# Residual of the down pass in five parts, recurrence rows loaded during attention, gate transposes in the other bank ring

## The chip, the cores and the metric

The kernel runs on one core of a Trainium2 chip. The core has five engines with an instruction stream each: TensorE (PE, matrix products), VectorE (DVE), ScalarE (ACT), GpSimd (POOL) and SyncE (SP), which here issues the DMA transfers. The metric is the device time of one execution in microseconds, the median over several runs.

## The reference

Two layers of a flow-matching backbone over 1024 latent tokens and a prefix of 256 context tokens, each of width 1024. In each layer half of the heads are a bidirectional matrix-memory recurrence (mLSTM) with its own gates, and half are a two-dimensional neighbourhood attention; both read one combined input projection and share one output projection. A squared-ReLU MLP with 4096 hidden features follows. Cut to what matters:

```python
for l in range(DEPTH):                                   # 2 layers
    need_ctx = l < DEPTH - 1                             # the context is not needed after layer 0
    h  = rmsnorm(x, norm1_g[l]) * (1.0 + sc1) + sh1      # scales and shifts from c (or c_ctx)
    hc = rmsnorm(xc, norm1_g[l]) * (1.0 + sc1c) + sh1c
    y, yc = token_mixers(h @ w_in[l], hc @ w_in[l], ...) # y: recurrence rows, then attention rows
    x = x + g1 * (y @ w_out[l])
    h = rmsnorm(x, norm2_g[l]) * (1.0 + sc2) + sh2
    x = x + g2 * (square(relu(h @ w_mlp1[l])) @ w_mlp2[l])
    # the same for xc with yc, if need_ctx
return rmsnorm(x, final_g)
```

In the recurrence, the gates of all tokens (four per head: input and forget, forwards and backwards) are accumulated along the tokens before anything can be weighted by them.

## The kernel before, in words

All products are made in three parts: each fp32 operand is split into a rounded part (`hi`, an ACT cast) and the rest (`lo`, a subtraction on DVE or POOL), and `mm3` (L94 to L96) adds hi x hi, hi x lo and lo x hi. Features lie on the 128 partitions, tokens along the free axis. The 1280 tokens are three groups: group 0 is the context (256 tokens), groups 1 and 2 are 512 latent tokens each. A product over the 1024 features takes eight k-tiles.

PSUM banks come from two rings: `mm` with 2 banks and `q` with 6, taken by `bank(tag)`. Whoever takes the next bank of a ring waits until its last reader is done. SBUF tiles come from pools in the same way: `wraw` (2 buffers) takes weights and rows as they land, `yraw` (2 buffers) takes rows during attention, and `raw` (6 buffers) takes the operands of the down pass. Within each engine, instructions run in a fixed order that a scheduler derives from the order in which the code is written; only the opening is ordered by hand.

A layer goes through these stages:

- **Keys, values and gates.** `mlstm_kv` projects tile by tile; ACT copies the values out of the bank (`va`, L497), DVE rotates the keys (L450 to L454), PE transposes them (L507). `gates` transposes the gate rows (L318) in three groups of 4, 4 and 2 tiles, and DVE adds the biases (L319, L320). From there a chain on DVE and ACT leads through the scans to `wc` (L364) and `st` (L374), which PE reads in L384 and L394. Value products of the attention heads stand between L318 and L384 on PE and cover the chain.
- **Recurrence, then attention.** The recurrence's output rows are stored to memory (`yscr`), k-tiles 0 to 3; attention's rows are k-tiles 4 to 7. Attention runs over pairs of heads and query tiles: scores (L986, L996), a fused maximum on DVE (L991, L997), the exponential on ACT (L1001), scaling on DVE (L1003), transposes on PE (L1014, L1025, L1038), copies by ACT and DVE, and the products with the values (L1048). Between these pieces the generator `ahead` already makes half of the output projection of the first group: it loads the group's rows with `load_y` (a DMA, an ACT cast at L1057, a subtraction at L1058) and runs four output tiles with a `residual` each (L1062). The first group is group 0 in layer 0, group 1 in layer 1.
- **Output projection.** `outproj` loads the eight k-tiles of each remaining group by `load_y` through `wraw`, then the weights of the output projection through the same two buffers.
- **Up and down.** The MLP uses products of sums of operands (seven instead of eight, named "1" to "7"). The down pass `run` goes through 56 steps in layer 0 (seven products of eight steps); each step is 24 matmuls of 512 columns, and operands are prepared four steps ahead (`AHEAD = 4`): DMA into `raw`, cast (L1098) and subtraction (L1099). At step 2 the function `load` brings in the whole residual `x` from memory (`xmid`), in pieces of 0.5 MB (context) and 1 MB (latent). The last step of each product adds banks to the residual (`take`): the first product needs the first half of group 1's features at step 7, the second needs the second half of group 2's at step 15, the third needs group 2's first half and group 1's second at step 23, and the context needs its own at the end.

The lines quoted are numbered as in the profile.

Of the kernel before, what the change touches and what calls it, by code (L numbers as in the profile page):

```python
# [26 lines left out]
KT = D // 128  # L27
# [10 lines left out]
def fview(a):  # L38
    return a.bitcast(F32)
# [8 lines left out]
class Kern:  # L48
# [81 lines left out]
    def load(self, pool, name, shape, src=None):  # L130
        t = pool.tile(shape, F32, name=name)
        self.nc.sync.dma_start(t[:], self.d[name] if src is None else src)
        return t
# [171 lines left out]
    def gates(self, l, tp_):  # L305
        nc, d = self.nc, self.d
# [6 lines left out]
        yield  # L313
        for c0 in range(0, NT, 4):
            nch = min(4, NT - c0)
            acc, ts = self.bank("mm"), slice(c0 * 128, (c0 + nch) * 128)
            for c in range(nch):
                nc.tensor.transpose(acc[:, c * 128:(c + 1) * 128], self.gr[:, c0 + c, :, :].rearrange("p q h -> p (q h)"), self.ident)  # L318
            nc.vector.tensor_scalar(ig[:, ts], acc[0:64, :nch * 128], self.bgate[l][:, 0:1], None, ALU.add)  # L319
            nc.vector.tensor_scalar(fg[:, ts], acc[64:128, :nch * 128], self.bgate[l][:, 1:2], None, ALU.add)  # L320
            yield
# [67 lines left out]
        for si, st in ((1, st2), (0, st1)):  # L389
            for c0 in range(0, NT, 4):  # L390
                nch = min(4, NT - c0)
# [499 lines left out]
    def ahead(self, l, gi, xsrc, yh, yl, W, xt):  # L891

        g0, n = GROUPS[gi]
        raw = []

        def fetch():
            raw.append(self.wp.tile([128, 1024], F32, name="wraw", bufs=WRAW))
            self.nc.sync.dma_start(raw[-1][:], self.d["w_out"][l, len(raw) - 1])

        for _ in range(WRAW):  # L900
            fetch()
        yield
        for i in range(WB):
            W.append(self.split_raw(raw[i], 1024))
            if len(raw) < WB:
                fetch()
            self.load_y(l, gi, yh, yl, range(2 * i, min(2 * i + 2, KT - 1)), self.np_)
            yield
        for f in range(WB):
            t = self.ap.tile([128, 512], F32R, name="ah2", bufs=KT)  # L910
            xt.append(fview(t[:, :n]))
            self.nc.sync.dma_start(xt[f], xsrc[f * 128:(f + 1) * 128, g0:g0 + n])
        self.load_y(l, gi, yh, yl, range(KT - 1, KT), self.np_)
        yield
        for f in range(WB):
            self.residual(gi, f, self.out_tile(f, gi, yh, yl, W[f]), 16, self.mod, xt[f])
            yield

    def out_tile(self, f, gi, hi, lo, w):
# [131 lines left out]
    def load_y(self, l, gi, hi, lo, ks=range(KT), pool=None):  # L1051
        nc = self.nc
        g0, n = GROUPS[gi]
        for k in ks:
            y = pool.tile([128, 512], F32, name="yraw", bufs=2) if pool else self.wp.tile([128, 1024], F32, name="wraw", bufs=WRAW)
            nc.sync.dma_start(y[:, :n], self.yscr[l][k * 128:(k + 1) * 128, g0:g0 + n])
            nc.scalar.copy(hi[k][gi][:], y[:, :n])  # L1057
            (nc.vector if gi == 2 or k == KT - 1 else nc.gpsimd).tensor_sub(lo[k][gi][:], y[:, :n], fview(hi[k][gi][:]))  # L1058

    def residual(self, gi, f, acc, row, mod, xs):  # L1060
        v = 1 if gi == 0 else 0
# [7 lines left out]
    def outproj(self, l, x, xsrc, groups, hi, lo, W=(), xt=()):  # L1069

        done = groups[0] if xt else -1
        for f0 in range(0, KT, WB):
            W = list(W) if f0 == 0 else []
            for gi in groups:
                if f0 == 0:
                    if gi == done:
                        self.load_x(x, xsrc, (gi,), (1,))
                        for f, t in enumerate(xt):
                            self.nc.scalar.copy(xf(x, gi, f), t)
                        continue  # L1080
                    self.load_y(l, gi, hi, lo)
                    self.load_x(x, xsrc, (gi,))
                if not W:
                    run_all(self.w_out(l, f0, W))
                for f in range(f0, f0 + WB):
                    self.residual(gi, f, self.out_tile(f, gi, hi, lo, W[f - f0]), 16, self.mod, xf(x, gi, f))
                    yield
# [255 lines left out]
    def down(self, l, hid, we, alloc):  # L1343

        nc, d = self.nc, self.d
# [111 lines left out]
        def run(x, mod, load, after, filler):  # L1457
            todo = iter(())
            for n in range(4, AHEAD):
                prepare(n)  # L1460
            for n, (p, b, s) in enumerate(whole):
                if n == 2:
                    load()
                if s == 0:
                    banks[p] = banks[ONTO[p]] if p in ONTO else [self.bank("mm") for _ in range(4)]
                w, h = ready.pop(n)
                for z in range(2):
                    for f in range(4):
                        multiply(banks[p][f][:], f, w[z], h[z], 512, p not in ONTO and s == z == 0, s == NS - 1 and z == 1)
                prepare(n + AHEAD)  # L1470
                next(todo, None)
                if n > 2 and n % 2:
                    next(filler, None)
                if s == NS - 1:
                    for f in range(4):
                        take(p, x, mod, f)
                    if p in "72":
                        run_all(todo)
                        alloc(2 if p == "7" else 1)
                        todo = after(2 if p == "7" else 1, 0, 512)  # L1480
            if not final:
                context(x, mod, todo, filler)
                alloc(0)
                run_all(after(0, 0, GROUPS[0][1]))
                return

            p, b = SEQUENCE[-1]
            banks[p], W, H = [self.bank("mm") for _ in range(4)], {}, {}

            def halves(o, k0):  # L1490
                r = raw()
                nc.sync.dma_start(r[:].rearrange("p (j t) -> p j t", j=4), hid["b"][HID.index(b), k0:k0 + 4, :, o:o + 256].rearrange("j p t -> p j t"))
                for z in range(4):
                    k = k0 + z
                    H[o, k] = (act("ah0", 256), act("al0", 256)) if o and k < KT else (act("ah1"), act("al1"))
                    self.parts(r[:, z * 256:z * 256 + 256], H[o, k][0][:, :256], H[o, k][1][:, :256])

            def chunk(i):
                halves(0, 4 * i)
                for s in (2 * i, 2 * i + 1):  # L1500
                    W[2 * s], W[2 * s + 1] = weights(p, s, s < 4)

            chunk(0)
            for i in range(4):
                if i < 3:
                    chunk(i + 1)
                for k in range(4 * i, 4 * i + 4):
                    for f in range(4):
                        multiply(banks[p][f][:, 0:256], f, W[k], H[0, k], 256, k == 0, k == 15)
                    next(todo, None)  # L1510
            run_all(todo)
            for i in range(4):
                halves(256, 4 * i)
            for f in range(4):
                take(p, x, mod, f, 0, 256)
            todo = after(1, 0, 256)
            q = self.bank("mm")

            def square(f, first=False, stop=False):
                sq = self.sp.tile([128, 512], F32, name="tmp", bufs=self.ntmp)  # L1520
                nc.scalar.activation(sq[:, :256], xf(x, 1, f, 256, 256), AF.Square)
                nc.tensor.matmul(q[:, :256], self.ones[:], sq[:, :256], start=first, stop=stop)

            for f in range(4):
                for k in range(16):
                    multiply(banks[p][f][:, 256:], f, W[k], H[256, k], 256, k == 0, k == 15)
                    if k % 4 == 3:
                        next(todo, None)
                square(f + 4, f == 0)
                if f:  # L1530
                    square(f - 1)
                take(p, x, mod, f, 256, 256)
            square(3, stop=True)
            run_all(todo)
            run_all(after(1, 256, 256, (q, 256)))
# [176 lines left out]
    def run(self):  # L1712
        nc, d = self.nc, self.d
        PS = bass.MemoryType.PSUM
        with self.open(name="pad", side="right") as pad, self.open(name="const") as self.cp, self.open(name="w") as self.wp, \
# [13 lines left out]
            hi, lo = self.alloc_act()  # L1729
# [3 lines left out]
            for l in range(DEPTH):  # L1733
                need_ctx = l < DEPTH - 1
                groups = (0, 1, 2) if need_ctx else (1, 2)
                yh, yl, W, xt = self.mixers(l, xsrc, hi, lo, need_ctx, W, accs, Wv if l == 0 else [])
# [82 lines left out]
                with self.open(name=f"xd{l}") as xp, self.open(name=f"sd{l}") as self.sp, self.open(name=f"we{l}") as wx:  # L1819
# [1 line left out]
                    self.wide, self.ntmp = 1, 3  # L1821
                    x = self.alloc_x(xp, groups)

                    def load():
                        self.load_x(x, xmid, groups)

                    if l == DEPTH - 1:
                        finish(x, mod, load, lambda *a: self.final(x, *a), ada)
# [66 lines left out]

RAWS = 6
AHEAD = 4
HID = ("11", "21", "22", "T1", "T2", "T3", "T4")


# [109 lines left out]
```

## Time and profile before

| | |
|---|---|
| median of 3 runs | 2866.62 us (2863.16 to 2868.66) |
| the profiled execution's own time | 2864.0 us |
| its span | 2862.2 us |
| mean granted clock of PE | 0.996 |
| PE busy | 2812.3 us (98%) |
| DVE, ACT, POOL busy | 2206.3 us (77%), 1267.9 us (44%), 105.4 us (4%) |
| DMA | 497.40 MB, mean 174 GB/s |

Every time stamp is counted in microseconds from the start of the span. A row of the timeline gives start, duration, engine, line, operation, what it writes and reads, and in brackets the idle time of the engine before it with what ended it. Gaps of PE are where time can be won or lost; the other engines count only where PE waits for them. The table's GB/s is a mean: in some stages the transfers stand at several times zero or near their highest rate, so a stage has to be looked at by itself.

### The profile page before, as it was taken

Reading aid. Unit: us, or ns where it says so; the run is one execution under the profiler, and the core shown is the slowest. Engines: PE = TensorE matmul, PEld = TensorE weight load, DVE = VectorE, ACT = ScalarE, POOL = GpSimd, SP = SyncE. Lnnn points to the kernel's source line nnn. Section 1 sums busy time; section 2 is a strip of 40 time slices with the busy share of each in tenths; the row PEclk is TensorE's granted clock in tenths of the full one; section 3 lists DMA queues with packets and bytes.
Section 4 is the critical chain, followed back from the end, with each engine's and each line's share of the span. In section 5 each row is a group of like instructions: output and inputs, shape, how many; then the busy total and the mean of one; then the engine's idle time right before and its main releaser. Section 6 shows DMA issues by size and latency. Waiting matters only on the chain. (4 is left out here: it accounts for less than half of the span.)

```text
span 2862.2 us, 45475 instructions
## 1 busy us (share of the span) xinstructions
PE 2812.3 (98%) x16500; PEld 2376.9 (83%) x16500; DVE 2206.3 (77%) x4917; ACT 1267.9 (44%) x2472; POOL 105.4 (4%) x183
## 2 busy tenths in 40 slices
PE   7999999999999999999999999999999999999998
PEld 4877788889888888888889988888887788888888
DVE  6779988776798777589878768878776887759774
ACT  5333335564553333344545333336555533334443
POOL 1110000010000000000000101000010000000000
PEclk9999999999999999999999999999999999999999
DMA  7433433246446555798977222223346354479672
GB/s 257 145 107 126 144 97 104 91 121 203 152 158 234 189 197 199 262 324 290 327 257 263 72 76 88 71 72 120 119 134 205 129 184 154 145 264 312 211 249 99
DMA packets 279264, 497.40 MB, mean 174 GB/s; under 512 B 23648, under 2 KB 119904, under 8 KB 279040
## 3 DMA queue, kind: packets, MB, share of 16 engines
q1 hardware_dynamic: 279040, 494.50, 51.8%
q8 instruction: 130, 2.13, 0.3%
q14 instruction: 94, 0.77, 0.1%
HBM read 398.82 MB, written 95.59 MB: 173 GB/s over the span
## 5 line engine op out<-in xcount | busy, mean ns | idle before, releaser
L94 PE MATMUL q<-ah,whi 128*128 128x512 f32 (+1 forms) x1472 | 549.9, 374 | 3.3 <-ACT ah L1098 2.7
L96 PE MATMUL q<-ah,wlo 128*128 128x512 f32 (+1 forms) x1472 | 547.4, 372 | 0.8 <-DVE wlo L1099 0.7
L95 PE MATMUL q<-al,whi 128*128 128x512 f32 (+1 forms) x1472 | 548.1, 372 | 0.0
L94 PE MATMUL mm<-ah,whi 128*128 128x512 f32 (+1 forms) x1120 | 387.6, 346 | 2.3 <-ACT whi L88 2.1
L96 PE MATMUL mm<-ah,wlo 128*128 128x512 f32 (+1 forms) x1120 | 385.4, 344 | 0.5 <-DVE wlo L89 0.5
L95 PE MATMUL mm<-al,whi 128*128 128x512 f32 (+1 forms) x1120 | 385.3, 344 | 0.0
L94 PEld LDWEIGHTS q<-ah,whi 128*128 128x128 f32 x1472 | 277.8, 189 | 53.2 <-ACT ah L1098 3.4
L96 PEld LDWEIGHTS q<-ah,wlo 128*128 128x128 f32 x1472 | 277.5, 189 | 50.4 <-DVE wlo L1099 1.7
L95 PEld LDWEIGHTS q<-al,whi 128*128 128x128 f32 x1472 | 277.7, 189 | 48.8 <-issue 1.4
L94 PE MATMUL mm<-whi,ah 128*128 128x512 f32 (+2 forms) x864 | 314.6, 364 | 0.4 <-DVE st L320 0.4
L95 PE MATMUL mm<-wlo,ah 128*128 128x512 f32 (+2 forms) x864 | 307.7, 356 | 0.6 <-DVE wlo L89 0.4
L96 PE MATMUL mm<-whi,al 128*128 128x512 f32 (+2 forms) x864 | 307.5, 356 | 0.0
L94 PEld LDWEIGHTS mm<-ah,whi 128*128 128x128 f32 x1120 | 212.5, 190 | 30.4 <-ACT whi L88 2.5
L96 PEld LDWEIGHTS mm<-ah,wlo 128*128 128x128 f32 x1120 | 212.4, 190 | 26.0 <-DVE wlo L89 1.0
L95 PEld LDWEIGHTS mm<-al,whi 128*128 128x128 f32 x1120 | 212.4, 190 | 25.1 <-issue 0.2
L1098 ACT CAST ah<-raw 128x512 fp32r<-128x512 f32 (+1 forms) x264 | 142.8, 566 | 120.4 <-PE q L96 53.5
L94 PEld LDWEIGHTS mm<-whi,ah 128*128 128x128 f32 x864 | 163.7, 189 | 27.7 <-issue 2.5
L96 PEld LDWEIGHTS mm<-whi,al 128*128 128x128 f32 x864 | 163.7, 189 | 23.2
L95 PEld LDWEIGHTS mm<-wlo,ah 128*128 128x128 f32 x864 | 163.9, 190 | 22.0 <-DVE wlo L89 1.4
L1099 DVE TENSOR_TENSOR al<-raw,ah 128x512 fp32r<-128x512 f32 (+1 forms) x264 | 157.6, 621 | 22.6 <-ACT ah L1098 22.3
L1099 DVE TENSOR_TENSOR wlo<-raw,whi 128x1024 fp32r<-128x1024 f32 x84 | 102.5, 1222 | 74.4 <-ACT whi L1098 71.7
L94 PE MATMUL q<-th,whi 128*128 128x512 f32 x384 | 150.4, 392 | 2.1 <-DVE s L1263 2.0
(306 smaller groups left out, 5232.9 us busy)
## 6 DMA issues: line engine op xcount, KB each, us to landing
raw<-w SPq DMA_DIRECT2D x168, 512.0 KB
raw<-hid SPq DMA_DIRECT2D x104, 512.0 KB
wada<-w_adaT SPq DMA_DIRECT2D x96, 512.0 KB
wraw<-w SPq DMA_DIRECT2D x80, 512.0 KB
hid<-hb SPq DMA_DIRECT2D x128, 256.0 KB
hid<-ht SPq DMA_DIRECT2D x96, 256.0 KB
w<-gscr SPq DMA_DIRECT2D x36, 512.0 KB
wada<-w_ada SPq DMA_DIRECT2D x32, 512.0 KB
```

The source lines that it names most:

```text
L94: mm(out, lh, rh, start=start, stop=False, skip_group_check=True)
L95: mm(out, lh, rl, start=False, stop=False, skip_group_check=True)
L96: mm(out, ll, rh, start=False, stop=stop, skip_group_check=True)
L1098: ins = self.nc.scalar.copy(hi, src)
L1099: self.nc.vector.tensor_sub(lo, src, fview(hi))
```

## The change

Three edits, and a table `LOADS` for the third.

- In `gates`, the transposes of the gate rows take their bank from the ring of six (`q`) and not from the ring of two (`mm`).
- In `ahead`, each of the four residuals is followed by one `load_y` for group 2: k-tiles 0 to 3, the recurrence's rows, go through `yraw` during attention, and their subtraction is on POOL. The output projection then loads only k-tiles 4 to 7 of group 2. This is in both layers.
- In the down pass, `load` takes a group and halves, and is called at five steps: at 2 the first half of group 1, at 12 the second half of group 2, at 14 its first half, at 16 the second half of group 1, at 18 the context (which layer 1 does not have).

```diff
@@ gates
-            acc, ts = self.bank("mm"), slice(c0 * 128, (c0 + nch) * 128)
+            acc, ts = self.bank(), slice(c0 * 128, (c0 + nch) * 128)
@@ ahead
         for f in range(WB):
             self.residual(gi, f, self.out_tile(f, gi, yh, yl, W[f]), 16, self.mod, xt[f])
+            self.load_y(l, 2, yh, yl, range(f, f + 1), self.np_)
             yield
@@ load_y
-            (nc.vector if gi == 2 or k == KT - 1 else nc.gpsimd).tensor_sub(lo[k][gi][:], y[:, :n], fview(hi[k][gi][:]))
+            (nc.vector if gi == 2 and k > 3 or k == KT - 1 else nc.gpsimd).tensor_sub(lo[k][gi][:], y[:, :n], fview(hi[k][gi][:]))
@@ outproj
-                    self.load_y(l, gi, hi, lo)
+                    self.load_y(l, gi, hi, lo, range(4 if gi == 2 else 0, KT))
@@ down, run
-                if n == 2:
-                    load()
+                if n in LOADS:
+                    load(*LOADS[n])
@@ run
-                    def load():
-                        self.load_x(x, xmid, groups)
+                    def load(gi, zs):
+                        if gi in groups:
+                            self.load_x(x, xmid, (gi,), zs)
@@ constants
+LOADS = {2: (1, (0,)), 12: (2, (1,)), 14: (2, (0,)), 16: (1, (1,)), 18: (0, (0, 1))}
```

How it moves instructions, at the three places of which the prediction speaks. Lines of the changed kernel are one to three higher behind `ahead`.

ACT at the end of layer 0's attention, before (`S` are score tiles, L1001 the exponential, `pc` and `pl3` copies of transposed scores, `ah` casts of rows):

```order
L1057 CAST ah0_4999<-yraw_7922 128x256
L1001 ACTIVATE S_7734,ssum_7753<-S_7734,smax_7747 128x520
L1057 CAST ah1_4997<-wraw_8349 128x512
L1001 ACTIVATE S_7735,ssum_7763<-S_7735,smax_7757 128x520
L1015 COPY pc_7811<-q_7810 128x512
L1015 COPY pc_7825<-q_7824 128x512
L1042 COPY pl3_7842<-q_7809 96x256
L1042 COPY pl3_7844<-q_7809 72x256
L1001 ACTIVATE S_7848,ssum_7867<-S_7848,smax_7861 128x544
L1001 ACTIVATE S_7849,ssum_7877<-S_7849,smax_7871 128x544
L1001 ACTIVATE S_7881,ssum_7900<-S_7881,smax_7894 128x640
```

The same place in the changed kernel, from the copy of `pc_7825` on:

```order
L1016 COPY pc_7825<-q_7824 128x512
L1043 COPY pl3_7842<-q_7809 96x256
L1043 COPY pl3_7844<-q_7809 72x256
L1058 CAST ah2_4983<-yraw_8109 128x512
L1002 ACTIVATE S_7848,ssum_7867<-S_7848,smax_7861 128x544
L1002 ACTIVATE S_7849,ssum_7877<-S_7849,smax_7871 128x544
L1002 ACTIVATE S_7881,ssum_7900<-S_7881,smax_7894 128x640
L1058 CAST ah2_4986<-yraw_8161 128x512
L1058 CAST ah2_4989<-yraw_8229 128x512
L1002 ACTIVATE S_7882,ssum_7910<-S_7882,smax_7904 128x640
L1016 COPY pc_7981<-q_7980 128x512
L1016 COPY pc_7995<-q_7994 128x512
```

The cast of row 0 (not shown) stands between the two exponentials of 520 columns, that of row 1 (`ah2_4983`) ahead of three exponentials, and those of rows 2 and 3 ahead of the fourth and two score copies.

PE at the gates of layer 1, before (`gr` are gate rows, `kt` keys, `mm_17014` a bank of value products):

```order
L507 MATMUL q_16936<-consts_153,kt_16826 128x128 x2
L318 MATMUL mm_16941<-consts_153,gr_16748 128x128 x4
L507 MATMUL q_16948<-consts_153,kt_16846 128x128 x2
L318 MATMUL mm_16970<-consts_153,gr_16748 128x128 x2
L507 MATMUL q_16953<-consts_153,kt_16923 128x128 x2
L94 MATMUL mm_17014<-whi_16960,ah0_16481 128x256
```

and changed, the first rows and, 16 value products left out, the rows where the last transposes now stand:

```order
L507 MATMUL q_16936<-consts_153,kt_16826 128x128 x2
L318 MATMUL q_16941<-consts_153,gr_16748 128x128 x4
L507 MATMUL q_16948<-consts_153,kt_16846 128x128 x2
L94 MATMUL mm_17014<-whi_16960,ah0_16481 128x256
L95 MATMUL mm_17014<-wlo_16961,ah0_16481 128x256
...
L94 MATMUL mm_17014<-whi_16966,ah0_16487 128x256
L507 MATMUL q_16953<-consts_153,kt_16923 128x128 x2
L318 MATMUL q_16970<-consts_153,gr_16748 128x128 x2
L95 MATMUL mm_17014<-wlo_16967,ah0_16487 128x256
```

Nineteen value products have moved ahead of the last key transposes and the last gate transposes; in layer 0 it is 21. L384 and L394 keep their place behind the same value products.

SP in the down pass of layer 0, before, behind the operands of step 5 (`x0`, `x1`, `x2` are the residual of the groups):

```order
L1412 DMA raw_12818<-hid0_81 128x2x512
L1570 DMA x0_12738<-xmid0_85 128x4x256
L1570 DMA x0_12739<-xmid0_85 128x4x256
L1570 DMA x1_12740<-xmid0_85 128x4x512
L1570 DMA x1_12741<-xmid0_85 128x4x512
L1570 DMA x2_12742<-xmid0_85 128x4x512
L1570 DMA x2_12743<-xmid0_85 128x4x512
L1364 DMA raw_12858<-w2 128x2x512
```

and changed, the same place, with the later parts after lines left out:

```order
L1413 DMA raw_12818<-hid0_81 128x2x512
L1571 DMA x1_12740<-xmid0_85 128x4x512
L1365 DMA raw_12853<-w2 128x2x512
...
L1571 DMA x2_12743<-xmid0_85 128x4x512
L1365 DMA raw_13337<-w2 128x2x512
...
L1571 DMA x2_12742<-xmid0_85 128x4x512
L1365 DMA raw_13428<-w2 128x2x512
```

One of six residual loads is left ahead of the operands of step 6; the other five stand each ahead of the operands that are prepared at their step, for four steps later.

## The prediction

> **What bounds the kernel now.** I read the shares of the engines first, then the table of PE's waits, then the stretches in which the granted clock falls below 1.00. The page's row of PE:
>
> ```profile
> PE 2812.3 (98%) x16500; PEld 2376.9 (83%) x16500; DVE 2206.3 (77%) x4917; ACT 1267.9 (44%) x2472; POOL 105.4 (4%) x183
> ```
>
> PE is busy in 2812.3 of 2862.2 us of span, so a change of the order of loads can win only from the 50 us in which PE idles, and from time in which PE runs at a lower clock. PE's waits in the profile, as releaser: total us, times, longest:
>
> ```profile
> PE mm L318 <- ACT va L497: 3.7, 3, 1.7
> PE q L94 <- ACT ah L1098: 2.7, 1, 2.7
> PE mm L94 <- ACT whi L88: 2.1, 1, 2.1
> PE q L507 <- DVE kt L454: 0.6, 2, 0.3
> PE mm L94 <- DVE st L320: 0.4, 1, 0.4
> ```
>
> The first, fourth and fifth are the gate stage (both layers), the second is the down pass of layer 0, the third the output projection of layer 1. These are the waits that the three edits touch; they add up to 9.5 us. Busy time by stretch (columns: stretch, length, then PE, PEld, DVE, ACT, POOL with counts, granted clock, DMA share, GB/s) shows what else hangs on them:
>
> ```profile
> 1200.00:1220.00 20.00, 17.25 (x70) 13.83 (x69) 5.61 (x8) 4.37 (x6) 0.00 (x0) 0.91 1.05 386
> 1620.00:1640.00 20.00, 19.12 (x144) 18.68 (x145) 18.25 (x14) 6.59 (x10) 5.52 (x6) 0.91 0.25 84
> 2180.00:2200.00 20.00, 19.02 (x75) 14.98 (x75) 11.23 (x12) 8.02 (x10) 0.00 (x0) 0.91 0.70 215
> ```
>
> A clock of 0.91 over 20 us is 0.09 x 20 = 1.8 us of lost PE time behind each of these three waits. So a wait of some 2 us costs nearly 4. The page "TensorE: Matmul & The Clock Gate" of the Trainium skill (Part 1) says the clock is halved only after at least one idle window of about 3.4 us, the windows running freely. By that rule none of these waits, the longest 2.75 us, would cost any clock, and the sum below would gain 3.6 us less; the 0.91 in the rows contradicts it, and I go by the rows. That the windows run freely would make a halving a matter of phase, not certain in each run.
>
> **Down pass, layer 0.** The relevant rows: SP's issues, PE's late step, and the supply of two later steps (the last split of a step's operand on DVE, and the step's first product on PE).
>
> ```profile
> 1190.09 9.91 SPq L1570 DMA_DIRECT2D x<-xmid  x6
> 1200.05 2.69 SPq L1364 DMA_DIRECT2D raw<-w  x1
> 1215.47 1.22 PE L94 MATMUL q<-ah,whi 128*128 128x512 f32 x2 [2.75 <-ACT ah L1098]
> 1264.70 1.29 DVE L1099 TENSOR_TENSOR al<-raw,ah 128x512 fp32r<-128x512 f32 x2 [0.52 <-ACT ah L1098]
> 1266.16 0.39 PE L94 MATMUL q<-ah,whi 128*128 128x512 f32 x1
> 1296.92 0.70 DVE L1099 TENSOR_TENSOR al<-raw,ah 128x512 fp32r<-128x512 f32 x1
> 1304.24 0.39 PE L94 MATMUL q<-ah,whi 128*128 128x512 f32 x1
> ```
>
> The six residual loads (5.2 MB) hold SP for 9.91 us and fill the DMA at 386 GB/s; the weights for step 6 are issued only at 1200.05 and reach PE 2.75 us late. The change leaves 1 MB in that place. The other 4.2 MB at 386 GB/s are 10.9 us, so step 6 is 8 us early instead: 2.75 + 1.8 = 4.55 us gained. What is put back, 1 MB each ahead of the operands of steps 16, 18, 20 and 22, is the danger: at step 15 before, the split ended at 1265.99 and PE began at 1266.16, a margin of 0.2; at step 22 it was 1304.24 - 1297.62 = 6.6. After, PE comes 4.6 earlier. Up to step 16 the supply has 10.9 us less ahead of it, so the margin grows to about 6; by step 22 all has been loaded and 6.6 - 4.6 = 2.0 is left. So I put what is given back at 0, with 0 to 2 us as bounds (2 if each megabyte's 2.7 us is late by a third of a step's 5.44 us, the seventh of 1304.24 - 1266.16). In layer 1 the same edit removes no wait of the table, and I put it at 0.
>
> **Output projection, layer 1.** First and last of the eight loads of recurrence and attention rows, the weight load behind them on SP, its split on ACT, and PE:
>
> ```profile
> 2153.32 0.32 SPq L1056 DMA_DIRECT2D wraw<-yscr  x1
> 2171.72 0.32 SPq L1056 DMA_DIRECT2D wraw<-yscr  x1
> 2174.76 2.63 SPq L74 DMA_DIRECT2D wraw<-w_out  x2
> 2179.36 1.04 ACT L88 CAST whi<-wraw 128x1024 fp32r<-128x1024 f32 x1 [0.94 <-DMA wraw<-w_out]
> 2180.46 0.50 PE L94 MATMUL mm<-ah,whi 128*128 128x512 f32 x1 [2.08 <-ACT whi L88]
> 2181.72 0.79 PE L96 MATMUL mm<-ah,wlo 128*128 128x512 f32 x1 [0.53 <-DVE wlo L89]
> ```
>
> Eight loads share two buffers, one every (2171.72 - 2153.32) / 7 = 2.6 us, and the weights wait for the same buffers. Four loads fewer put them 10.5 us earlier, and PE needs them only 2.1 earlier: both gaps go, and the clock's loss with them: 2.08 + 0.53 + 1.8 = 4.4 us. Layer 0 has no such wait in the table, so nothing is gained there.
>
> **Gate transposes.** With the wider ring PE no longer waits for the copy of the last tile's values, and goes on with value products. But the gates' own chain on DVE and ACT is not shortened, since its last input (the third group of transposes) is not earlier. PE meets it again in L384 (which reads wc) and L394 (which reads st). Layer 0, then layer 1:
>
> ```profile
> 110.12 1.27 ACT L374 ACTIVATE st<-st 64x1280 f32<-64x1280 f32 x1 [1.11 <-DVE st L372]
> 110.99 2.40 PE L394 MATMUL q<-consts,st 128*128 128x128 f32 x20
> 1620.12 0.44 PE L318 MATMUL mm<-consts,gr 128*128 128x128 f32 x2 [1.47 <-ACT va L497]
> 1645.19 0.19 ACT L364 ACTIVATE wc<-wc 64x10 f32<-64x10 f32 x1
> 1646.39 1.12 PE L384 MATMUL q<-wc,sel 64*64 64x10 f32 x32
> 1647.01 1.27 ACT L374 ACTIVATE st<-st 64x1280 f32<-64x1280 f32 x1 [1.11 <-DVE st L372]
> 1647.45 2.40 PE L394 MATMUL q<-consts,st 128*128 128x128 f32 x20
> ```
>
> In layer 0 PE comes 3.7 - 1.47 + 0.3 = 2.5 us earlier. The chain ends at 111.39; the transposes that read it are the second half of the x20 (from some 112.1), so 0.2 to 0.9 us can be kept: 0.5. In layer 1 PE comes 1.47 + 0.3 + 0.4 + 1.8 (clock) = 4.0 us earlier, but the chain ends at 1648.28 and its readers begin at about 1648.5: 0.2 is kept. The other 3 us (1646.39 - 4.0 = 1642.4, wc ready at 1645.38) become one wait ahead of L384, and that is as long as the waits which halved the clock; a new halving costs up to 1.8 behind it. I take a loss of 0.5, from a gain of 0.2 to a loss of 1.6.
>
> **Loads during attention.** Each load is a DMA, an ACT cast of 0.62 and a subtraction on POOL, which is 4% busy. They share two buffers with the first group's rows. What such a cast does ahead of other work is in these rows of layer 0 (ACT, PE, then the place where the new ones go):
>
> ```profile
> 627.33 0.62 ACT L1057 CAST ah<-wraw 128x512 fp32r<-128x512 f32 x1 [2.37 <-DMA wraw<-yscr]
> 629.81 0.38 PE L986 MATMUL q<-nk,nqc 128*128 128x256 f32 x1 [1.17 <-ACT pc L1015]
> 654.47 1.33 POOL L1058 TENSOR_TENSOR al<-wraw,ah 128x512 fp32r<-128x512 f32 x1 [3.79 <-ACT ah L1057]
> 656.22 0.42 DVE L1058 TENSOR_TENSOR al<-yraw,ah 128x256 fp32r<-128x256 f32 x1
> 659.33 0.75 ACT L1001 ACTIVATE S<-S,smax 128x544 f32<-128x544 f32 x1 [0.29 <-DVE smax L997]
> 661.59 0.60 PE L1014 MATMUL q<-consts,S 128*128 128x128 f32 x4
> ```
>
> ACT waited 2.37 for rows to land, and PE 1.17 behind it. In the changed order the cast of row 1 stands ahead of three exponentials, of which the row at 659.33 is the second. Its buffer is freed at 656.64; with a landing time of 3.5 (below) ACT is held to 660.1 + 0.6, so after the first of them the second begins near 661.5, some 2 us late. Between its end (660.08) and the transposes at 661.59 lay 1.5 us, part of it DVE's scaling; I take the transposes to be 1.3 late. The casts of rows 2 and 3 stand ahead of the next exponential and of two score copies; row 3's buffer waits for POOL's 1.33 us on row 1, so it lands near 665.5: another 1 to 2 us. I take 2.7 us plus 0.3 for a halved clock, bounds 1 and 5. In layer 1 (SP, ACT, ACT, PE):
>
> ```profile
> 2128.76 0.33 SPq L1056 DMA_DIRECT2D yraw<-yscr  x1
> 2132.55 0.62 ACT L1057 CAST ah<-yraw 128x512 fp32r<-128x512 f32 x1 [1.16 <-DMA yraw<-yscr]
> 2137.79 0.64 ACT L1042 COPY pl<-q 128x256 f32<-128x256 f32 x2 [0.29 <-PE q L1038]
> 2143.10 0.66 PE L1048 MATMUL q<-pc,vc 128*64 128x128 f32 x8
> ```
>
> The landing takes 2132.55 - 2129.09 = 3.5. Two casts land ahead of the copies at 2137.79, one behind the other, which moves their end from 2138.4 to about 2141.3; PE reads them at 2143.10. So 0, at most 1. "DMA: Bandwidth & Descriptors" of the Trainium skill (Anatomy of one DMA) gives, for DMAs issued by GpSimd, a fixed 2.0 us plus the bytes' time, an estimate of 2.6 us for 256 KB; this trace shows 3.5 here, and by 2.6 the loss in layer 0 would be some 1 us less.
>
> **Sum**, against the profiled execution of 2864.0 us: -4.5 -4.4 -0.5 +0.5 +3.0 +0 = -5.9, or 2858.1. The median of the runs, 2866.62, stands 2.6 above the profiled one, so 2860.7 on that scale. A difference of 0.2% (5.7 us) is what can be told from no change; the sum lies on that edge.
>
> **Rivals.**
> - The gain stands whole (20%): the casts find their rows landed, ACT's 44% leaves room, and layer 0's attention loses nothing. -8.9, 2857.7. Against it speaks the buffer freed only at 656.64. If the gate chain too were faster than I read it, -4.5 -4.4 -2.5 -4.0 = -15.4, 2851.2 (included, 5 of the 20).
> - The loads in attention cost more than all gains (11%): one mechanism, each row's load waiting for the buffer of the one before, and exponentials queued behind each landing. Three landings of 3.5 in layer 0, three less the 4.7 of free time before 2143.10 in layer 1, and a halved clock after each: 10.5 + 5.8 + 3.6 = 19.9 against gains of 9.4, so +10.5: 2877. It decides from 15 us of stalls on; the one stall shown before, 1.17, speaks against it.
> - The parts collide with the supply of steps 16 to 22 (10%): the 4.5 are lost again, -1.4, 2865. For it: DVE's margin of 0.2 at step 15. Against: only 2.0 us of margin is needed.
> - The weights of the output projection do not follow the row loads, because the first buffers are held by something else (5%): -1.5, 2865.
>
> **Numbers.** The forecast has 54%; its own range, from the bounds of the terms, is 2857 to 2866, half of it below the edge of 2860.9. Faster: 27 + 20 = 47%. Slower by more than 0.2%: the second rival, 11%. The same: 42%. The range for 8 in 10 reaches to 2853 and, towards the second rival, to 2869.
>
> **What would show it.** Right: no wait of PE on ah near 1215; no wait of L94 on whi behind the last row of loads in layer 1, and a clock of 1.00 in both stretches; L318 out of PE's waits but L384 or L394 waiting for wc or st; in layer 0's attention end ACT idle for yraw and PE for S or pc, 1 to 5 us. Wrong: L384 without a wait (the gates gain), a wait on ah or x at steps 15 to 23, or casts that find their rows there.

## The result, and the profile after

The changed kernel takes 2860.61 us (median of 20 runs, 2857.70 to 2865.33); the kernel before, run beside it 20 times, takes 2865.88 (2861.29 to 2873.24). The ratio is 0.9980, with a 95% interval of 0.9974 to 0.9987: 5.3 us, about 0.2%, faster, and the interval leaves out 1. The forecast was 2860.7 us. The profiled execution takes 2858.64 us with a span of 2856.7, against 2864.0 and 2862.2.

That a forecast lands so close says little of its terms, so they are taken one by one. Both kernels run 16500 matmuls, and outside the gates the change does not alter their order by more than a few places. So the n-th matmul of one trace can be compared with the n-th of the other, and its time after minus its time before is how far PE is ahead (negative) or behind at that place. What this number does between two places is what the stage between them won or lost. From the two first profiles:

| stage (matmul numbers) | forecast, us | measured, us |
|---|---|---|
| start to gates, layer 0 (0 to 200) | 0 | -0.4 |
| gates, layer 0 (200 to 750) | -0.5 | -1.1 |
| recurrence and attention, layer 0 (750 to 4150) | 0 | 0.0 |
| end of attention, layer 0 (4150 to 4500) | +3.0 | +2.6 |
| output projection and up, layer 0 (4500 to 7200) | 0 | +0.1 |
| down, layer 0 (7200 to 7600) | -4.5 | -4.6 |
| rest of layer 0, gates of layer 1 (7600 to 9850) | +0.5 | +1.8 |
| recurrence and most of attention, layer 1 (9850 to 12700) | 0 | 0.0 |
| end of attention, layer 1 (12700 to 13275) | 0 | +0.9 |
| output projection, layer 1 (13275 to 13500) | -4.4 | -4.7 |
| up, down, final | 0 | 0.0 |
| sum (of the unrounded) | -5.9 | -5.5 |

PE's waits in the changed kernel (columns as before):

```profile
PE q L384 <- ACT wc L364: 3.3, 1, 3.3
PE q L1015 <- DVE S L1004: 3.2, 8, 0.7
PE q L394 <- ACT st L374: 1.5, 1, 1.5
```

The waits of L318, of L94 on `ah` and on `whi` of the output projection are gone from the table. In their place stand two waits for the gates' chain, 3.3 us in layer 1 and 1.5 in layer 0. PE's wait for score tiles (L1015, L1014 before) is 3.2 us instead of 1.9, but e1 below, which has none of the new loads, has 3.1: this total alone does not show what they cost. Busy time by stretch, the three stretches that answer to those shown of before:

```profile
1200.00:1220.00 20.00, 20.00 (x90) 16.55 (x89) 14.31 (x21) 9.43 (x16) 0.00 (x0) 1.00 0.97 358
1640.00:1660.00 20.00, 18.12 (x172) 17.79 (x173) 14.26 (x40) 6.86 (x14) 0.40 (x5) 0.83 0.36 110
2170.00:2190.00 20.00, 20.00 (x90) 16.57 (x89) 10.89 (x12) 8.29 (x10) 0.00 (x0) 1.00 0.64 212
```

PE is busy throughout in the down pass and in the output projection, at full clock. In the gates of layer 1 the clock fell further than before, to 0.83 over 20 us. The timeline of ACT and PE there:

```profile
1641.63 0.20 ACT L364 ACTIVATE wc<-wc 64x10 f32<-64x10 f32 x1
1641.88 1.90 PE L384 MATMUL q<-wc,sel 64*64 64x10 f32 x32 [3.27 <-ACT wc L364]
1643.71 4.39 PE L394 MATMUL q<-consts,st 128*128 128x128 f32 x20
```

PE stood 7.9 us ahead of before when it reached L384, and waited 3.27 for `wc`. Behind that wait the 32 small products take 1.90 us instead of 1.12 and the 20 transposes 4.39 instead of 2.40: halved clock. Of the 7.9 us, 6.1 are gone by the end of the stage.

The end of layer 0's attention, rows of POOL, SP, ACT and PE:

```profile
653.15 1.28 POOL L1059 TENSOR_TENSOR al<-yraw,ah 128x512 fp32r<-128x512 f32 x1 [3.85 <-ACT ah L1058]
654.46 0.32 SPq L1057 DMA_DIRECT2D yraw<-yscr  x1
658.48 0.62 ACT L1058 CAST ah<-yraw 128x512 fp32r<-128x512 f32 x1 [1.79 <-DMA yraw<-yscr]
661.12 0.44 PE L1015 MATMUL q<-consts,S 128*128 128x128 f32 x2 [0.68 <-DVE S L1004]
663.12 0.62 ACT L1058 CAST ah<-yraw 128x512 fp32r<-128x512 f32 x1 [0.23 <-DMA yraw<-yscr]
665.09 0.62 PE L997 MATMUL q<-nk,nq 128*128 128x384 f32 x2 [0.57 <-ACT pc L1016]
```

The load of row 1 is issued as soon as POOL has done row 0 (654.43), lands 3.7 us after its issue (654.78 to 658.48), and holds ACT for 1.79; three exponentials stand behind that cast. PE then waits for their scaled scores, and at 665.09 for a score copy (`pc`) that stands behind the casts of rows 2 and 3.

### The profile page after: what moved, and what is told of

Its sections match the earlier page's. It is cut to its first block, busy times and chain, and to the rows that moved or that the text cites. A ratio compares the mean times of both kernels' runs of the same rounds, so it can differ in the third digit from the quotient of the medians.

```text
span 2856.7 us, 45490 instructions
## 1 busy us (share of the span) xinstructions
PE 2808.0 (98%) x16500; PEld 2375.7 (83%) x16500; DVE 2204.9 (77%) x4909; ACT 1268.7 (44%) x2472; POOL 116.5 (4%) x191
## 5 line engine op out<-in xcount | busy, mean ns | idle before, releaser
L94 PE MATMUL q<-ah,whi 128*128 128x512 f32 (+1 forms) x1472 | 549.3, 373 | 1.2 <-ACT whi L1099 1.2
L94 PE MATMUL mm<-ah,whi 128*128 128x512 f32 (+1 forms) x1120 | 386.8, 345 | 0.2 <-DVE nq L846 0.2
L94 PEld LDWEIGHTS q<-ah,whi 128*128 128x128 f32 x1472 | 277.4, 188 | 51.0 <-ACT whi L1099 2.1
L94 PE MATMUL mm<-whi,ah 128*128 128x512 f32 (+2 forms) x864 | 314.0, 363 | 0.0
L94 PEld LDWEIGHTS mm<-ah,whi 128*128 128x128 f32 x1120 | 212.0, 189 | 27.9 <-issue 2.0
L94 PEld LDWEIGHTS mm<-whi,ah 128*128 128x128 f32 x864 | 163.0, 189 | 26.7 <-issue 1.6
L94 PE MATMUL q<-th,whi 128*128 128x512 f32 x384 | 149.8, 390 | 2.1 <-DVE s L1264 2.0
L95 PE MATMUL q<-x,whi 128*128 128x512 f32 x384 | 149.9, 390 | 1.1 <-DVE x L1100 1.1
```

The costliest lines, as they stand in the source:

```text
L94: mm(out, lh, rh, start=start, stop=False, skip_group_check=True)
L95: mm(out, lh, rl, start=False, stop=False, skip_group_check=True)
```

## The experiments

Comparisons of time are with runs of the kernel before on the same chip, and kernels of one group share these. The chips differ: the kernel before had medians of 2869.2 (e1 to e4), 2869.8 (e5 to e8) and 2871.2 us (e9 to e11), so numbers of different groups aren't subtracted. Where a stage is given in us, it is counted by matmul numbers as above, against the first profile of before.

### e1, e2, e3: each edit alone

Each is the kernel before with one edit of the change: only `LOADS`, only the bank of the gate transposes, only the rows loaded during attention.

> Before with only the five-part residual. Theory (the six residual loads ahead of step 6 made the wait of 2.75 us and the halved clock behind it, and the later parts are covered): PE has no wait on ah near 1215, the clock stays at 1.00 there, PE stands 4.6 us earlier from step 7 on, nothing is lost at steps 15 to 23 nor in layer 1; time 4.6 us below before. Rival (the later parts collide with the supply): a new wait of 1 to 4 us on ah or x at steps 16 to 23; time 0 to 3 us below before.

> Before with only the gate transposes in the ring of six. Theory (the gate chain takes over, and in layer 1 the long wait for it halves the clock): layer 0 gains about 1 us, layer 1 has a wait of 3.3 us ahead of L384 and a halved clock behind it and loses about 1.8; time 0.5 to 1 us above before. Rival (the wider ring is worth the waits it removes): PE gains 2.5 in layer 0 and 4.0 in layer 1; time 6.5 us below before.

> Before with only the recurrence rows of group 2 loaded during attention. Theory: layer 0's attention end loses 2.5 us, layer 1's 0.9, layer 1's output projection gains 4.7 (gaps of 2.08 and 0.53 and the halved clock gone); time about 1.3 us below before. Rival (the weights of the output projection come early for another reason, by the other edits): the wait on whi near 2178 stays, and the time is 3 us above before.

| | median, us | ratio to before (95%) | difference, us | expected |
|---|---|---|---|---|
| e1, down alone | 2863.43 | 0.9980 (0.9971 to 0.9989) | -5.8 | -4.6 |
| e2, gates alone | 2869.77 | 1.0000 (0.9992 to 1.0009) | +0.6 | +0.5 to +1 |
| e3, rows alone | 2868.46 | 0.9998 (0.9989 to 1.0007) | -0.7 | -1.3 |

They add up to -5.9. The down pass alone brings what the whole change brings; the other two edits together bring nothing that can be measured. The traces say why. In e1 the down stage is 4.64 us shorter, as in the change. In e2 the gates of layer 0 gain 0.9 and those of layer 1 lose 2.1, with the same waits as in the change:

```profile
PE q L384 <- ACT wc L364: 3.3, 1, 3.3
PE q L394 <- ACT st L374: 1.5, 1, 1.5
```

In e3 the wait for `whi` in layer 1's output projection is gone (-4.7), the end of attention costs 3.2 in layer 0 and 1.2 in layer 1. The rivals of e1 and e2 (a collision; a gain of 6.5) are out. In e3 the interval, -3.2 to +2.0 us, holds the expected -1.3 and only just leaves out the rival's +3; the trace decides: the rows alone remove the wait.

Two numbers did not fit. In e2, which still loads the residual in one go, the down stage of layer 0 is 2.7 us shorter than in the first profile of before: PE waits for `ah` at step 6 for 1.64 us instead of 2.75, and the clock stays at 1.00. And in e1 and e2, which have the wait in the output projection of layer 1, that stage is 1.9 and 2.3 us shorter than in the first profile of before. In e1 PE still waits 1.64 and 0.53 there, but the clock is not halved behind it (last row, 1.00):

```profile
2181.85 0.50 PE L94 MATMUL mm<-ah,whi 128*128 128x512 f32 x1 [1.64 <-ACT whi L88]
2183.11 0.50 PE L96 MATMUL mm<-ah,wlo 128*128 128x512 f32 x1 [0.53 <-DVE wlo L89]
2180.00:2200.00 20.00, 17.83 (x76) 13.94 (x76) 11.73 (x13) 8.32 (x10) 0.00 (x0) 1.00 0.71 209
```

So some 2 of the 4.7 us won in this stage are not lost in each execution of before. In e1 0.4 of them are the shorter wait (1.64 instead of 2.08), the rest is clock. e9 comes back to this.

### e4: a buffer of its own, and the wide ring in layer 0 only

```diff
-            acc, ts = self.bank(), slice(c0 * 128, (c0 + nch) * 128)
+            acc, ts = self.bank("mm" if l else "q"), slice(c0 * 128, (c0 + nch) * 128)
...
-            y = pool.tile([128, 512], F32, name="yraw", bufs=2) if pool else self.wp.tile([128, 1024], F32, name="wraw", bufs=WRAW)
+            y = pool.tile([128, n], F32, name="yraw7", bufs=1) if pool and n == 256 and k == KT - 1 else pool.tile([128, 512], F32, name="yraw", bufs=2) if pool else self.wp.tile([128, 1024], F32, name="wraw", bufs=WRAW)
```

> The change with two differences: the gate transposes use the ring of six in layer 0 alone, and the last row tile of the context group has its own 1 KB buffer, so that the four new loads of layer 0 do not wait for its subtraction and are issued some 20 us earlier. Theory (the shared buffer made the stall in layer 0; the wait for the gate chain cost the clock in layer 1): layer 0's attention end loses less than 0.8 us instead of 2.5, layer 1's gates lose 0 instead of 1.8; time 3.5 us below the change, 9 us below before. Rival (ACT's casts themselves delay attention, and the clock is a matter of chance): no difference from the change, within 1 us.

Measured: 2862.85 us, ratio 0.9976 (0.9965 to 0.9986), 6.3 us below before instead of 9. By the time alone the rival (no difference from the change) fits. The stages tell more. The half on the gates came true: the gates of layer 1 end 0.2 ahead of before instead of 1.8 behind. The half on layer 0's attention fell: that stage loses 5.6 us, more than in the change. With the buffer free the scheduler put all four loads some 20 us earlier, and the casts of rows 2 and 3 ahead of score copies of an earlier pair (ACT, ACT, PE, then the stretch):

```profile
638.44 0.62 ACT L1058 CAST ah<-yraw 128x512 fp32r<-128x512 f32 x1 [0.83 <-DMA yraw<-yscr]
640.49 0.62 ACT L1058 CAST ah<-yraw 128x512 fp32r<-128x512 f32 x1 [1.43 <-DMA yraw<-yscr]
641.64 1.22 PE L987 MATMUL q<-nk,nq 128*128 128x256 f32 x4 [3.35 <-ACT pc L1016]
635.00:655.00 20.00, 16.65 (x140) 15.36 (x138) 13.89 (x44) 11.62 (x24) 9.07 (x7) 0.83 0.57 165
```

The same mechanism at another place: a cast that waits for its load holds the copies behind it on ACT, PE waits 3.35 for one of them, and the clock is halved behind that. The shared buffer set where the stall fell, not whether there was one.

### e5 to e8: the change again, a variant, and two tests

> The changed kernel itself, on the chip of the next three, as their base. Theory (the ledger of the two first profiles): 5.3 us below before; layer 1's gates wait about 3.3 us for wc with a halved clock behind it, layer 0's attention end loses 2.5 us. Rival (the gain belonged to one chip): within 2 us of before.

> The change without the recurrence rows of layer 0 during attention (layer 0 loads all eight k-tiles in the output projection, as before) and with the gate transposes in the ring of six in layer 0 alone. Theory (each edit pays in one layer only): layer 0's attention end loses 0 instead of 2.5, layer 1's gates 0 instead of 1.8; time 4.3 us below the change, 9.6 below before. Rival (layer 0's output projection needs the early rows once PE is earlier): a new wait of 2 us on whi in layer 0's output projection; time 1 us below the change or less.

> The change with 28 transposes of a constant (some 3 us, their output unused) ahead of L384 in layer 1, so that PE is not idle while it waits for wc. Theory (the idle time halves the clock, and without that the gates' chain alone sets the time): clock 1.00 at 1640 to 1660, a wait of about 1 us for st at L394, layer 1's gates lose 0 instead of 1.8; time 1.8 us below the change. Rival (the halving is no consequence of the wait, or the extra work costs what it saves): no difference, or 1 us above the change.

> The change with the later residual loads bunched at steps 12, 13 and 14 (2 MB, 1 MB, 1 MB) instead of 12, 14, 16 and 18. Theory (each megabyte takes 2.7 us of the supply; the margins before were 2.6 at step 17 and 3.2 at step 18, and PE is 4.6 us earlier): a wait of 1.5 to 2 us on ah at step 17 or 18, perhaps with a halved clock behind it; time 1.5 to 4 us above the change. Rival (the six buffers hold enough, the margins are larger than read): no wait; same time as the change.

| | median, us | ratio to before (95%) | difference to e5, us |
|---|---|---|---|
| e5, the change | 2862.71 | 0.9976 (0.9967 to 0.9985) | |
| e6, variant | 2860.97 | 0.9967 (0.9954 to 0.9979) | -1.7 |
| e7, PE kept busy | 2861.39 | 0.9971 (0.9960 to 0.9983) | -1.3 |
| e8, parts bunched | 2863.99 | 0.9980 (0.9970 to 0.9989) | +1.3 |

The intervals of the ratios overlap: none of the differences in the last column is clear of what the runs vary by.

e5 is the change itself: 7.1 us below before on this chip. The gain did not belong to the first chip alone.

**e6** has the rows during attention in layer 1 only, and the wide ring in layer 0 only:

```diff
+            acc, ts = self.bank("mm" if l else "q"), slice(c0 * 128, (c0 + nch) * 128)
...
-            self.load_y(l, 2, yh, yl, range(f, f + 1), self.np_)
+            if l:
+                self.load_y(l, 2, yh, yl, range(f, f + 1), self.np_)
...
-                    self.load_y(l, gi, hi, lo, range(4 if gi == 2 else 0, KT))
+                    self.load_y(l, gi, hi, lo, range(4 if gi == 2 and l else 0, KT))
```

(`load_y` also subtracts on DVE again for all of group 2 in layer 0.) Expected were 4.3 us below the change; the medians say 1.7. In its trace layer 1's gates end 0.2 ahead of before, as expected, and layer 0's output projection has no new wait. The end of layer 0's attention loses 1.3 where 0 was expected (in e1, also without these loads, it loses 1.1). e10 and e11 measure the variant again.

**e7** is the change with 28 transposes of a constant in front of L384 in layer 1, whose result nobody reads:

```diff
         p = self.bank()
+        for _ in range(28 if l else 0):
+            nc.tensor.transpose(p[:, 128:256], self.ident, self.ident)
         for h in range(8):
```

They fill the wait; PE's timeline (L382 are the added ones, L386 is L384 of before, L396 is L394), and the stretch:

```profile
1642.18 3.22 PE L382 MATMUL q<-consts 128*128 128x128 f32 x28
1645.88 1.12 PE L386 MATMUL q<-wc,sel 64*64 64x10 f32 x32 [0.48 <-ACT wc L364]
1646.93 1.31 PE L396 MATMUL q<-consts,st 128*128 128x128 f32 x10
1648.77 2.27 PE L396 MATMUL q<-consts,st 128*128 128x128 f32 x10 [0.53 <-ACT st L374]
1640.00:1660.00 20.00, 18.99 (x190) 18.18 (x189) 14.36 (x31) 6.79 (x14) 0.40 (x5) 0.91 0.22 64
```

Two waits of 0.5 are left, and still the clock was halved for a while (0.91), now behind the small products. The stage (7600 to 9850, the added ones left out) lost 1.3 us here and 0.6 in e5. So keeping PE busy in the profile's sense did not keep the clock up. That the halving goes with idle time is shown by the rows under e9; what else than idle time counts, and whether the products of 10 columns do here, stays open.

**e8** bunches the later parts of the residual:

```diff
-LOADS = {2: (1, (0,)), 12: (2, (1,)), 14: (2, (0,)), 16: (1, (1,)), 18: (0, (0, 1))}
+LOADS = {2: (1, (0,)), 12: (2, (0, 1)), 13: (1, (1,)), 14: (0, (0, 1))}
```

No wait came: the down stage is 4.64 us shorter than before, as in the change. My theory fell. The margins, by the last split of a step's operands on DVE and the step's first product on PE, at step 22 of the change, and at step 18 of e8:

```profile
1288.66 1.28 DVE L1100 TENSOR_TENSOR al<-raw,ah 128x512 fp32r<-128x512 f32 x2
1300.70 0.39 PE L94 MATMUL q<-ah,whi 128*128 128x512 f32 x1
```

```profile
1276.72 1.29 DVE L1100 TENSOR_TENSOR al<-raw,ah 128x512 fp32r<-128x512 f32 x2
1279.50 0.39 PE L94 MATMUL q<-ah,whi 128*128 128x512 f32 x1
```

In the change it is 1300.7 - 1289.9 = 10.8 where 2.0 were forecast, and it is 7.7 or more at each of the steps 15 to 22; in e8 the smallest margin is 1.5 at step 18 where -1.5 was expected. The price of the bunch was right: its margin falls from 9.7 at step 15 to 1.5 at step 18, by 8.2, while before it grew by 3.0 over these steps (0.2 to 3.2), which makes 11.2 us for 4 MB, where 2.7 us each give 10.9. Wrong was the margin to start from. Spread out, the parts cost less, and the transfers' rate says why. The same stretch before and in the change:

```profile
1260.00:1280.00 20.00, 20.00 (x90) 16.53 (x90) 17.89 (x31) 10.41 (x19) 0.00 (x0) 1.00 0.91 308
```

```profile
1260.00:1280.00 20.00, 20.00 (x90) 16.57 (x89) 17.67 (x30) 8.94 (x16) 0.00 (x0) 1.00 1.04 391
```

Before, the transfers ran at 308 GB/s there, and with residual loads among them they can run at 391. Before, they were not at their limit, so a megabyte put there by itself did not cost the operands its full 2.7 us.

### e9 to e11: before once more, and the variant against the change

> The kernel before once more, for its trace. Theory (the windows of the clock run freely, so the same waits are halved in one execution and not in another): the same waits as in the first profile near 1213, 1619 and 2178, of 1 to 3 us each, but at least one of them without a halved clock behind it; Rival (a wait of 2 us always halves the clock): all three show 0.91 over 20 us.

> The changed kernel, more runs beside the next one. All theories: 5 to 7 us below before.

> The change with the rows of group 2 during attention in layer 1 alone, and the wider ring for gate transposes in layer 0 alone, more runs beside the change. Theory (layer 0's rows cost 1.5 to 4.5 us according to the clock, layer 1's wider ring 0.8 to 2): 2 to 4.5 us below the change, 8 to 10 below before. Rival (the two differences are within what varies from run to run): less than 1.5 us below the change.

e9 is the kernel before, one execution (2868.84 us). PE waits at the same three places, first the down pass, then the gates of layer 1 and the output projection (PE's timeline, then the stretches behind the waits):

```profile
1218.93 1.22 PE L94 MATMUL q<-ah,whi 128*128 128x512 f32 x2 [3.75 <-ACT ah L1098]
1624.06 0.44 PE L318 MATMUL mm<-consts,gr 128*128 128x128 f32 x2 [1.47 <-ACT va L497]
1624.81 0.44 PE L507 MATMUL q<-consts,kt 128*128 128x128 f32 x2 [0.32 <-DVE kt L454]
1625.69 0.36 PE L94 MATMUL mm<-whi,ah 128*128 128x256 f32 x1 [0.44 <-DVE st L320]
2184.78 0.50 PE L94 MATMUL mm<-ah,whi 128*128 128x512 f32 x1 [1.26 <-ACT whi L88]
2186.04 0.50 PE L96 MATMUL mm<-ah,wlo 128*128 128x512 f32 x1 [0.53 <-DVE wlo L89]
1215.00:1235.00 20.00, 16.25 (x61) 13.09 (x61) 14.08 (x21) 7.53 (x12) 0.00 (x0) 0.83 0.92 328
1622.00:1642.00 20.00, 17.77 (x146) 17.09 (x145) 18.26 (x18) 6.42 (x12) 5.51 (x6) 1.00 0.29 93
2184.00:2204.00 20.00, 18.69 (x73) 14.91 (x74) 10.75 (x12) 7.78 (x10) 0.00 (x0) 0.91 0.69 210
```

In the gates of layer 1 the waits are those of the first profile (1.47, 0.32 and 0.44), the clock was 0.91 then and is 1.00 now. Behind the shorter wait of the output projection (1.26 + 0.53) it was halved. So a wait of about 2 us halves the clock in one execution and not in the next; the rival (always) is out.

The traces show what decides it. In every profile the granted clock changes only at the marks of a grid of 3.41 us, which lies elsewhere in each execution, and it is halved for one or two whole windows between marks. Two windows in a row, first for the gates of layer 1 (the first profile of before, then e9), then for the output projection (e9, then e1):

```profile
1618.23:1621.64 3.41, 1.30 (x8) 0.59 (x6) 3.35 (x8) 1.17 (x4) 0.00 (x0) 1.00 0.67 198
1621.64:1625.06 3.42, 3.31 (x15) 3.34 (x16) 3.37 (x4) 2.02 (x3) 1.50 (x2) 0.50 0.30 114
1620.10:1623.51 3.41, 2.49 (x21) 2.25 (x19) 2.65 (x4) 2.50 (x5) 0.00 (x0) 1.00 0.15 25
1623.51:1626.93 3.42, 2.12 (x14) 1.67 (x15) 3.31 (x8) 0.91 (x3) 0.61 (x1) 1.00 0.80 275
2183.30:2186.71 3.41, 1.62 (x6) 0.88 (x6) 1.92 (x2) 1.04 (x1) 0.00 (x0) 1.00 0.71 214
2186.71:2190.13 3.42, 3.42 (x10) 2.67 (x9) 1.85 (x2) 1.04 (x1) 0.00 (x0) 0.50 0.51 160
2178.07:2181.49 3.42, 2.14 (x10) 1.45 (x8) 2.04 (x3) 1.63 (x3) 0.00 (x0) 1.00 0.85 233
2181.49:2184.90 3.41, 2.52 (x10) 1.78 (x11) 1.23 (x1) 1.30 (x2) 0.00 (x0) 1.00 0.58 199
```

The columns are those of the stretches above. Where all or nearly all of the waits fall into one window, PE is busy there for 1.30 or 1.62 us, and the next window is halved (0.50). Where a mark cuts them, PE is busy for more than 2 us on both sides, and no window is halved. From 45 us after the start to 2840, the thirteen profiles have 20 windows at full clock in which PE is idle for 1.85 us or more; all 20 are followed by a halved one. Of some 10,500 with less idle time 7 are, the least idle of them the one ahead of the halving in e7 (0.87 us; it holds products of 10 columns).

| | median, us | ratio to before (95%) |
|---|---|---|
| e10, the change | 2863.08 | 0.9973 (0.9964 to 0.9982) |
| e11, variant of e6 | 2859.41 | 0.9964 (0.9950 to 0.9977) |

The variant is 3.7 us below the change here, within the expected 2 to 4.5, and 1.7 in the group before. Taken together (20 runs of the change, 10 of the variant) the medians are 2862.9 and 2860.2, 2.7 apart; a resampling of these runs gives 1.0 to 5.0 for the difference. It is the fastest of the kernels run here, by about 0.1%. What the stages did in the executions profiled, in us against the first profile of before:

| stage | before again (e9) | change | e5 | e10 | variant e6 | e11 |
|---|---|---|---|---|---|---|
| gates, layer 0 | +1.5 | -1.1 | -1.2 | -1.2 | -1.1 | -1.0 |
| end of attention, layer 0 | +0.2 | +2.6 | +5.7 | +3.8 | +1.3 | +0.7 |
| down, layer 0 | +1.8 | -4.6 | -4.6 | -4.6 | -4.6 | -4.6 |
| to the end of the gates, layer 1 | -0.5 | +1.8 | +0.6 | +2.2 | -0.2 | -0.3 |
| end of attention, layer 1 | +1.5 | +0.9 | +2.0 | +0.9 | +1.7 | +2.1 |
| output projection, layer 1 | -0.7 | -4.7 | -4.7 | -4.7 | -4.7 | -4.7 |

Where PE has no wait, a stage comes out the same to a tenth in these executions (-4.6, -4.7). Where it waits, the stage varies by 1 to 3 us. A halved window, 3.41 us at half clock, is 1.7 of that: in e5 the end of layer 0's attention cost 5.7, since behind waits of 1.25 and 0.38 the clock was halved for two windows, with most of the wait of 1.05 in the first of them (0.83 over 20 us):

```profile
661.99 0.44 PE L1015 MATMUL q<-consts,S 128*128 128x128 f32 x2 [1.25 <-DVE S L1004]
664.97 0.66 PE L1015 MATMUL q<-consts,S 128*128 128x128 f32 x2 [1.05 <-DVE S L1004]
660.00:680.00 20.00, 17.32 (x140) 16.21 (x137) 14.93 (x50) 11.02 (x25) 3.82 (x3) 0.83 0.42 133
```

## Why the prediction was right, and where not

The forecast held: 2860.7 against 2860.61, and the likeliest case came with its signs. That the two agree to 0.1 us is luck: the terms are off by up to 1.3 us and cancel to 0.4, and the profiled executions stand at different places among the runs (2.6 us below the median of the three runs before, 2.0 below that of the 20 after). Point by point:

- **Down pass, layer 0** (-4.5 forecast, -4.6 measured, and alone -5.8 in e1). The mechanism and its size held: one load instead of six ahead of step 6, no wait, full clock. What failed is a step beside it: the margins of steps 16 to 22, worked out as if each megabyte pushed back all later operands by 2.7 us (bunched in e8 it did, spread out it did not). It took the supply before as running at the transfers' limit, which the 308 GB/s of that stretch against 386 in the stall could have told. The margin was 10.8 instead of 2.0, and even the bunch of e8 caused no wait. The rival of a collision deserved less than its 10%. The size holds against the first profile of before: with the old loads this stage took 2.7 us less in e2, 0.1 less in e3 and 1.8 more in e9, so the change saves 2.0 to 6.5 there by execution.
- **Output projection, layer 1** (-4.4, -4.7). Right, and shown by e3. But the size holds against the first profile of before only: some 2 us of it, most of them the halved clock, are not lost in e1 and e2.
- **Gates** (-0.5 and +0.5, -1.1 and +1.8). That PE would meet the chain again was right, with the wait at 3.27 where 3 was forecast, and e2 and e4 show it from both sides. The mis-sized term is the clock in layer 1: 0.5 of loss was taken, 1.6 was the bound, and 1.8 was measured, 0.6 and 2.2 in other executions. The halving lasted for two windows, not one as behind the waits of the first profile of before (0.83 over 20 us, not 0.91). In layer 0 the gain was under-sized: 0.9 was my upper bound and 1.1 was measured.
- **End of attention, layer 0** (+3.0, +2.6). The mechanism was right: ACT holds exponentials and score copies behind casts that wait for their loads. Two inputs were wrong and partly cancelled: row 1's buffer is the one that POOL frees with row 0 (at 654.43 in this trace), 0.9 us earlier than the one that I named (freed at 655.32), and from there the cast began 4.05 us later, not 3.5. The size is in part luck: in this execution the clock was not halved there. Where it was (e10, e7, e5), the stage lost 3.8, 5.3 and 5.7, above the upper bound of 5 in two of three; the 0.3 put down for the clock was too little.
- **End of attention, layer 1** (0, +0.9). The bound was 1. The cases without these loads (e1: +2.0, e2: +2.2, e9: +1.5) show the same stage vary by more, so that the loads cost anything there isn't shown. With them e4 and e8 lost the most, 4.5 and 3.4, with a halved window in each.
- The rival in which the chain takes nothing (-15) and the one in which the loads cost more than all gains (+10) did not come. Nor did the output projection fail to follow.

So two of three edits paid in one layer each, and lost in the other what they had won there: the wide ring gains about 1 in layer 0 and costs about 1.5 in layer 1 (+0.6 to +2.2 in the profiles with it, -0.5 to +0.6 in those without); the rows cost layer 0 about 3 (2.6 to 5.7 in the profiles with them, 0 to 1.3 in those without) and spare layer 1 between 2.4 and 4.7. This is why e2 and e3 measure as nothing, and why the variant of e6 and e11 is below the change.

## What to carry to other kernels

A wait that is removed is worth only what the next thing behind it allows: before counting it, find the chain that PE meets next and how much slack it has there. An edit that is made in all layers has to be priced in each; here two edits were worth having in one layer only. On an engine that works in order, a cast of freshly loaded data is a wait for that load placed in front of all that follows, so put it where the load has landed, not where its issue is free.

## What the runs showed of the hardware

- Whether a wait of some 2 us halves the clock depends on where it lies against a grid of 3.41 us, which is another in each execution (rows under e9). The same waits in the gates of layer 1 (2.2 us in all) had a clock of 0.91 in the first profile of before and 1.00 in e9; waits of 1.26 and 0.53 were halved in e9, and 1.64 and 0.53 in e1 weren't. The wait of 3.3 us for the gates' chain had a lowered clock in all its profiles: 0.83 (the change, e2, e10) or 0.91 (e5, e8). By these rows a halving costs 1.7 us (one window at half clock) or 3.4 (two), and that much varies between executions; these two are estimates from the length of the windows. The page "TensorE: Matmul & The Clock Gate" of the Trainium skill (Part 1) calls for an idle window of about 3.4 us before the clock falls. That the windows run freely agrees with these rows, that a whole one has to be idle does not.
- Transposes of a constant that kept PE busy for 3.22 us (e7) did not keep the clock up: it fell behind 32 products of 10 columns and two waits of 0.5 us. What counts as busy stays open.
- Transfers moved 391 GB/s in a stretch of the down pass in which they had moved 308 before, without any step being late.
